# Two transformer blocks on one core: squares summed as tiles become final, the context normed beside an FFN, and a block's start woven tile by tile

## The chip, the core and the metric

The kernel runs on one core of a Trainium2 chip. The metric is the device time of one execution in microseconds (us); a few runs are made and the median is given. Beside the runs stands one profiled execution, from which every row below is read. Engines are written as the profile writes them: PE is TensorE's matmul, PEld its weight load, DVE VectorE, ACT ScalarE, POOL GpSimd, SP SyncE (which issues most transfers). PEclk is TensorE's granted clock as a share of full speed.

## What is computed

One sequence x of 512 tokens and 1024 channels passes through two blocks, all in float32. The first block has four layers, each a mixer and a gated FFN, each behind a root-mean-square norm over the channels:

```
def rmsnorm(x, g):
    return x * rsqrt(mean(x * x, axis=-1) + 1e-6) * g

for i in range(4):          # mixers: hyena, window attention, pooling, hyena
    x = x + mixer_i(rmsnorm(x, norm_mix[i]))
    x = x + (silu(h @ w_gate) * (h @ w_up)) @ w_down      # h = rmsnorm(x, norm_ffn[i])
```

The hyena mixer has a projection, a short convolution, and two long convolutions that are done by Fourier transforms, with the filters' spectra made by a small network. The second block works on x and on a context of 256 further tokens:

```
h  = rms(x,   norm_attn) * (1 + mod_x[1]) + mod_x[0]     # mod_x, mod_c: from c and c_ctx
hc = rms(ctx, norm_attn) * (1 + mod_c[1]) + mod_c[0]
qkv, z, beta, decay, cq, ckv, k_rope, gates = split(h @ w_in)     # the same of hc
o_gdn = gated delta rule, 8 heads, both directions, chunks of 64 tokens
o_mla = softmax attention, 8 heads, keys and values from a low-rank ckv, queries from cq
x = x + mod_x[2] * ((sigmoid(g1) * (o_gdn' @ w_a) + sigmoid(g2) * (o_mla @ w_b)) @ w_out)
x = x + mod_x[5] * (relu(h2 @ w_mlp_in) ** 2 @ w_mlp_out)         # h2: normed and modulated x
```

## The kernel before

Everything is held with channels on the 128 partitions: x is eight tiles `self.x[k]` of [128 channels, 512 tokens] that stay in the on-chip memory. To keep float32 accuracy each operand of a product is split in a high and a low part, and each 128 x 128 block of weights meets a tile of activations in three matmuls (`mm`, lines 383 to 385: high x high, high x low, low x high). A product of one *part*, 128 output channels from eight tiles, is thus 24 matmuls.

Weights come through a plan. Each stage's `plan_...` method lists its requests in the order of their use (`want`, `want_cols`); `part()` takes the next and lets `ahead()` (lines 350 to 375) load the following ones on SyncE's queue and split them: the high part is a cast on ScalarE (L371), the low part a difference on VectorE (L372). There are two buffers for split parts (`look` is 1), so while one is used the next is made. `mark()` ends the stretch of the plan that is loaded ahead before the buffers change size.

The program is written by generators that yield estimates of the TensorE time that they have emitted. `weave` runs several of them side by side, each at an even share of its total, and a scheduler then orders the instructions of each engine by that order and by what is ready.

The stages follow each other: hyena 0, FFN 0 (with the modulation vectors beside it), attention, FFN 1, pooling, FFN 2 (with the second hyena's filters beside it), hyena 3, FFN 3, and `second`, which holds the whole second block: context and x normed, the gate scalars, eight heads of the delta rule (`gdn`), latent attention (`mla`), `merge` and `mlp`.

What the change touches, with the lines of the profile:

- *Norms.* `rstd_g` (L408 to 429) squares eight tiles on ScalarE (L415, L418), adds them on VectorE into `acc` (L419), sums over the channels by a matmul with ones (L422), and takes the root on ScalarE (L425) and the reciprocal on VectorE (L428). The pools of some stages give the sums other names (`raw`, `tmp`, `u`). In the first block `normed` multiplies by the gain at once, and the row factor is wanted only after the first products; in the second block `modulated` (L1151 to 1168) needs the row factor first, then makes each tile by two VectorE instructions and one on ScalarE (L1161, L1165, L1166).
- *Products into x.* `add_to_x` (L501) adds a finished product to x; the FFN's last stretch is eight such products from `hs`, at most eight tiles. L496 is the FFN's gating on GpSimd.
- *Start of the second block.* `second` norms the context first, then x, then runs `both` (a product of a part for x and the context) for a part of 96 columns, turns the result (L1247), computes `gate_scalars` (L1302 to 1349) and only then enters `gdn`. There `front(h)` is a head's projections with short convolution (`gdn_proj`; head 0's keys, values, queries in this order; L1425 turns keys) and `gdn_prep`; `inverse` makes the triangular inverses and `gdn_scan` the recurrence:

```
run(front(0))
weave((self.inverse(tl, own(0, 2), st[0], c), INV + LAG), (front(1), FRONT))
```

- *Last MLP.* `mlp` norms x by `modulated`, then runs 32 parts, of which the squared ReLU goes to the second product.
- *Latent attention.* `keys(hp, out)` makes keys and values of two heads: a product, a norm with a table load on ScalarE (L449), the scaling of each key tile on VectorE (L1767, and the rope part on GpSimd L1768), and the turning of scaled tiles by TensorE (L1776). It is woven with the logits and the values of the heads before (L1837, L1862, L1866).
- *First hyena.* `hyena` opens a pool for the projections and, inside it, the pool of the convolution; L815 loads the spectra `kd` of the filters, L771 stores projections to `vd`, and `kd<-K` is the store of the spectra.

## Time and profile before

| | before |
|---|---|
| median of 3 runs | 4254.73 us (4250.41 to 4256.73) |
| span of the profiled execution | 4239.0 us, 48425 instructions |
| mean granted TensorE clock | 0.962 |
| busy: PE, PEld | 94%, 76% of the span |
| busy: DVE, ACT, POOL | 59%, 37%, 21% |
| DMA | 421.82 MB, mean 100 GB/s |

The span runs from the first to the last instruction of the profiled execution; of that execution only the span is known, and the three runs were made without a profile. A start time in a row is counted from the span's start. Weight loads overlap matmuls, so PE and PEld are not added. In a timeline a bracket behind an instruction gives the idle time of its engine before it and what ended that time.

### The profile page before, as it was taken

The numbers are of one execution on the slowest core, as the hardware profiler recorded it, in microseconds if no ns is written. First come the engines' busy times: TensorE is split into PE (matmuls) and PEld (weight loads), VectorE is DVE, ScalarE is ACT, GpSimd is POOL, SyncE is SP. The second block draws the span as 40 slices with busy tenths as digits, with TensorE's granted clock in tenths as the row PEclk, the third lists the DMA queues.
The fourth block names the chain that finished last, engine by engine and source line by source line (L and its number), as shares of the span: only waits on it lengthen the run. The fifth ranks groups of instructions, "written<-read, shape, count | busy, mean of one in ns | idle before, by whom it ended". The sixth has DMA issues, their size and how long they took to land. (4 is left out here: it accounts for less than half of the span.)

```text
span 4239.0 us, 48425 instructions
## 1 busy us (share of the span) xinstructions
PE 3972.3 (94%) x18340; PEld 3208.1 (76%) x18340; DVE 2511.9 (59%) x4171; ACT 1561.0 (37%) x2858; POOL 896.4 (21%) x977
## 2 busy tenths in 40 slices
PE   7988999989999989998998999689999989998999
PEld 5777788766788777877877888578888876676887
DVE  6766887468544465655666444567777665644333
ACT  4321322257422352323222222454444456643222
POOL 2544101111011102322332111023333321101111
PEclk9999999999999999999999999889999999999999
DMA  4542355230332223334431323222122111242222
GB/s 153 171 172 105 110 189 179 90 102 21 97 97 92 86 87 120 118 116 154 147 122 63 99 90 97 81 63 58 50 65 61 55 45 44 90 134 80 95 94 90
DMA packets 370770, 421.82 MB, mean 100 GB/s; under 512 B 20614, under 2 KB 337046, under 8 KB 365674
## 3 DMA queue, kind: packets, MB, share of 16 engines
q1 hardware_dynamic: 361514, 377.46, 28.1%
q0 software_dynamic: 8736, 40.93, 2.5%
q8 instruction: 144, 2.36, 0.2%
q14 instruction: 88, 0.72, 0.1%
q10 hardware_dynamic: 288, 0.34, 0.0%
HBM read 372.27 MB, written 44.32 MB: 98 GB/s over the span
## 5 line engine op out<-in xcount | busy, mean ns | idle before, releaser
L371 ACT CAST whi<-wraw 128x1024 fp32r<-128x1024 f32 (+4 forms) x546 | 533.3, 977 | 1428.7 <-PE ps L384 1270.3
L383 PE MATMUL ps<-xh,whi 128*128 128x512 f32 x1904 | 787.6, 414 | 15.4 <-ACT whi L371 15.4
L372 DVE TENSOR_TENSOR wlo<-wraw,whi 128x1024 fp32r<-128x1024 f32 (+4 forms) x546 | 676.4, 1239 | 185.0 <-ACT whi L371 165.9
L385 PE MATMUL ps<-xh,wlo 128*128 128x512 f32 x1904 | 760.3, 399 | 1.2 <-DVE wlo L372 1.1
L384 PE MATMUL ps<-xl,whi 128*128 128x512 f32 x1904 | 757.4, 398 | 0.0
L383 PEld LDWEIGHTS ps<-xh,whi 128*128 128x128 f32 x1904 | 361.4, 190 | 101.5 <-ACT whi L371 16.1
L385 PEld LDWEIGHTS ps<-xh,wlo 128*128 128x128 f32 x1904 | 360.2, 189 | 92.2 <-DVE wlo L372 3.7
L384 PEld LDWEIGHTS ps<-xl,whi 128*128 128x128 f32 x1904 | 361.2, 190 | 87.9 <-issue 4.9
L496 POOL TENSOR_TENSOR u<-u,a 128x512 f32<-128x512 f32 x88 | 152.5, 1735 | 1219.2 <-ACT whi L371 737.3
L383 PE MATMUL ps<-hh,whi 128*128 128x512 f32 x960 | 384.5, 400 | 3.0 <-ACT hh L311 3.0
L384 PE MATMUL ps<-hl,whi 128*128 128x512 f32 x960 | 381.0, 397 | 1.0 <-DVE hl L312 1.0
L385 PE MATMUL ps<-hh,wlo 128*128 128x512 f32 x960 | 380.7, 397 | 1.1 <-DVE wlo L372 1.1
L383 PE MATMUL ps<-act,whi 128*128 128x512 f32 (+1 forms) x688 | 291.0, 423 | 9.9 <-ACT act L1165 9.9
L384 PE MATMUL ps<-act,whi 128*128 128x512 f32 (+1 forms) x688 | 284.7, 414 | 1.1 <-DVE act L1166 0.9
L385 PE MATMUL ps<-act,wlo 128*128 128x512 f32 (+1 forms) x688 | 282.4, 411 | 0.0
L501 DVE TENSOR_TENSOR x<-x,ps 128x512 f32<-128x512 f32 x128 | 88.1, 688 | 218.0 <-PE ps L385 217.5
L383 PEld LDWEIGHTS ps<-hh,whi 128*128 128x128 f32 x960 | 180.9, 188 | 47.3 <-ACT hh L311 4.7
L384 PEld LDWEIGHTS ps<-hl,whi 128*128 128x128 f32 x960 | 181.0, 189 | 45.6 <-DVE hl L312 2.4
L385 PEld LDWEIGHTS ps<-hh,wlo 128*128 128x128 f32 x960 | 180.9, 188 | 45.1 <-DVE wlo L372 1.9
L383 PEld LDWEIGHTS ps<-act,whi 128*128 128x128 f32 (+1 forms) x688 | 134.6, 196 | 39.6 <-ACT act L1165 13.3
L574 PE MATMUL ps<-pg,fwd 128*128 128x256 f32 x512 | 133.4, 409 | 30.1 <-DVE pg L564 30.1
L385 PEld LDWEIGHTS ps<-act,wlo 128*128 128x128 f32 (+1 forms) x688 | 134.6, 196 | 30.3 <-issue 0.2
(538 smaller groups left out, 7103.9 us busy)
## 6 DMA issues: line engine op xcount, KB each, us to landing
wraw<-ff_w_gate SPq DMA_DIRECT2D x44, 1024.0 KB
wraw<-ff_w_up SPq DMA_DIRECT2D x44, 1024.0 KB
wraw<-ff_w_down SPq DMA_DIRECT2D x32, 1024.0 KB
wraw<-w_in SPq DMA_DIRECT2D x53, 512.0 KB
wraw<-hy_w_in SPq DMA_DIRECT2D x24, 1024.0 KB
w<-w_mod SPq DMA_DIRECT2D x24, 1024.0 KB
kd<-K POOLq DMA_DIRECT2D x16, 1152.0 KB, 4.8
K<-kd SPq DMA_DIRECT2D x16, 1152.0 KB
```

Of the source, the lines that this page charges most:

```text
L371: nc.scalar.copy(out=hi, in_=src)
L372: nc.vector.tensor_tensor(out=lo, in0=src, in1=hi.bitcast(F32), op=SUB)
L383: nc.tensor.matmul(out[:m, :cols], lhsT=whi[:, k, :m], rhs=xhi[:, :cols], start=(first and k == 0), stop=False)
L384: nc.tensor.matmul(out[:m, :cols], lhsT=whi[:, k, :m], rhs=xlo[:, :cols], start=False, stop=False)
L385: nc.tensor.matmul(out[:m, :cols], lhsT=wlo[:, k, :m], rhs=xhi[:, :cols], start=False, stop=(last and k == nk - 1))
L496: nc.gpsimd.tensor_tensor(out=u, in0=u, in1=a, op=MUL)
L501: self.nc.vector.tensor_tensor(out=self.x[j], in0=self.x[j], in1=ps, op=ADD)
L574: nc.tensor.matmul(ps[:, c, :], lhsT=self.fwd[:, t, s, c, :], rhs=st[t][s], start=(s == 0), stop=(s == 1))
```

## The change

- Each tile of x is squared when it becomes final (`final(j)`): ScalarE squares it, GpSimd adds it to `xsum`, and VectorE adds the last of eight. It is called from the last products of each FFN, the second half of the hyena's and of attention's output, the pooling mixer and the merge. `rstd_g` takes this sum where there is one. The two new tiles take the place of one pair of `h` buffers in FFN 2 (10 instead of 11).
- The context is loaded, normed and modulated by `context`, which runs beside FFN 3; a stage `open_second` before it opens the pools.
- `modulated` becomes a generator, and `modulated_first` takes the first two parts of the plan: it runs the context's products of both, then makes x's tiles one by one and puts the six matmuls of each (two parts, three each) behind it (`mm_k`). In the second block the two parts are the gate scalars' and head 0's keys', which the plan requests early; in the last MLP they are the first two of 32.
- The gate scalars are a generator that is woven with head 0's projections; several small transposes share one copy; the constants are loaded later. `gdn_prep` and `inverse` of head 0 are woven with the whole of head 1's `front`.
- `keys` of latent attention yields 5.0 between the scaling and the turning; the totals of two weaves are 25 and 13 instead of 20 and 10.
- In the first hyena the convolution's pool is opened after the projections' pool is closed.
- Docstrings and comments go; they are left out of the diff below.

```diff
+    def mm_k(self, out, wpart, k, x, last):
+        nc = self.nc
+        (whi, wlo, m), (xhi, xlo) = wpart, x
+        nc.tensor.matmul(out[:m, :], lhsT=whi[:, k, :m], rhs=xhi, start=(k == 0), stop=False)
+        nc.tensor.matmul(out[:m, :], lhsT=whi[:, k, :m], rhs=xlo, start=False, stop=False)
+        nc.tensor.matmul(out[:m, :], lhsT=wlo[:, k, :m], rhs=xhi, start=False, stop=last)
+
+    def final(self, j):
+        nc = self.nc
+        if self.xsums == 0:
+            self.xsum = self.xp.tile([P, T], F32, tag="xsum", name=self.nm("xsum"))
+            nc.scalar.activation(out=self.xsum, in_=self.x[j], func=AF.Square)
+        else:
+            sq = self.xp.tile([P, T], F32, tag="xsq", name=self.nm("xsq"))
+            nc.scalar.activation(out=sq, in_=self.x[j], func=AF.Square)
+            e = nc.vector if self.xsums == KD - 1 else nc.gpsimd
+            e.tensor_tensor(out=self.xsum, in0=self.xsum, in1=sq, op=ADD)
+        self.xsums += 1
+
+    def last_to_x(self, j, ps):
+        self.add_to_x(j, ps)
+        self.final(j)
+
     def rstd_g(self, xs, n, cols=T, tl=None):
...
-        acc = tl("acc", 1)
-        for k, x in enumerate(xs):
+        if xs is self.x and self.xsums == KD:
+            acc, self.xsums = self.xsum, 0
+        else:
+            acc = tl("acc", 1)
+            for k, x in enumerate(xs):
...
-                    hs.append(self.split(pool, u, "h", 11))
-            yield from self.proj(8, hs, self.add_to_x)
+                    hs.append(self.split(pool, u, "h", 10 if li == 2 else 11))
+            yield from self.proj(8, hs, self.last_to_x if g0 + gn == DFF // P else self.add_to_x)
...
+                if first is None:
+                    with self.pool("hy") as pool:
+                        self.hyena_conv(pool, s, first, inputs)
+            if first is not None:
                 with self.pool("hy") as pool:
                     self.hyena_conv(pool, s, first, inputs)
...
-            yield from self.proj(8, zs[k:k + 4], self.add_to_x if k else res)
+            yield from self.proj(8, zs[k:k + 4], self.last_to_x if k else res)
...
-            run(self.proj(8, list(zip(oh_, ol_))[4:], self.add_to_x))
+            run(self.proj(8, list(zip(oh_, ol_))[4:], self.last_to_x))
...
                 nc.vector.tensor_tensor(out=self.x[k], in0=self.x[k], in1=d, op=ADD)
+                self.final(k)
...
-        rstd = self.rstd(x, D, cols=cols)
-        xs = []
+        rstd = yield from self.rstd_g(x, D, cols)
+        xs = [] if xs is None else xs
...
             xs.append((hi, lo))
+            yield 1.0
         return xs
+
+    def modulated_first(self, x, mod, j0, gname, before=()):
+        parts, xs, before = [self.part() for _ in range(2)], [], list(before)
+        ps = [self.psum() for _ in parts]
+        n = 0
+        for _ in self.modulated(self.sx, x, mod, j0, gname, "act", xs=xs):
+            if before:
+                run(before.pop(0)(parts))
+            for k in range(n, len(xs)):
+                for p, part in zip(ps, parts):
+                    self.mm_k(p, part, k, xs[k], k == KD - 1)
+            n = len(xs)
+        return xs, ps
...
         self.want([(w[:, 4768:4832], 0), (w[:, 4096:4128], 64)], KD, 96, [[(0, 96)]])
+        self.want_cols(w, 0, KD, D, P, P)
...
-                if (h < 8) if c < 3 else (h > 0):
+                if (h < 8 and (h or c != 1)) if c < 3 else (h > 0):
...
+    def context(self, pool):
+        cx = []
+        for k in range(KD):
+            t = pool.tile([P, CX], F32, name=self.nm("cx"), tag=f"cx{k}")
+            self.nc.sync.dma_start(out=t, in_=self.i["ctxT"][k * P:(k + 1) * P, :])
+            cx.append(t)
+        yield 1.0
+        self.nt = pool
+        self.cs = yield from self.modulated(self.ctx2, cx, self.modc, 0, "norm_attn_2", "ctx", cols=CX)
+        self.nt = None
...
-            xs = self.modulated(self.sx, self.x, self.modx, 0, "norm_attn_2", "act")
+        with self.norm_pool():
+            pc = [self.psum() for _ in range(2)]
+            xs, px = self.modulated_first(self.x, self.modx, 0, "norm_attn_2",
+                                          [lambda parts, e=e: self.mm(pc[e], parts[e], cs, CX) for e in range(2)])
...
-        run(front(0))
-        weave((self.inverse(tl, own(0, 2), st[0], c), INV + LAG), (front(1), FRONT))
+        weave((self.gate_scalars(b2, lambda: tl([P, 6, P], "w", 7).rearrange("p c d -> p (c d)"), given[0], sc), 30),
+              (self.gdn_proj(tl, own, 0, xs, cs, got, zs, given[1]), 24.0))
...
+        def begin():
+            yield from self.gdn_prep(tl, own, 0, got, st, sc, c)
+            yield from self.inverse(tl, own(0, 2), st[0], c)
+        weave((begin(), 51.0), (front(1), FRONT))
...
         if h < 8:
-            yield from self.both(xs, cs, conv, 0, 2)
+            if given:
+                conv(0, *given)
+            yield from self.both(xs, cs, conv, 1 if given else 0, 1 if given else 2)
             yield from keys()
...
                         g.tensor_scalar(out=kq[:, c, e, :], in0=kr[:, c, :], scalar1=rk[:, c, e:e + 1], scalar2=None, op0=MUL)
+                yield 5.0
                 kT = [tl([P, TT], "kT", 4) for e in range(2)]
...
-            weave((scan, 16.0), (first(), 20.0))
+            weave((scan, 16.0), (first(), 25.0))
...
-                          (values(s - 1, m[(s - 1) // 2], got) if s else None, 8.0), (side, 10.0))
+                          (values(s - 1, m[(s - 1) // 2], got) if s else None, 8.0), (side, 13.0))
...
                                        op0=MUL, op1=ADD)
+                self.final(j)
             run(self.proj(8, zs, res))
...
-            xs = self.modulated(self.sx, self.x, self.modx, 24, "norm_mlp_2", "act")
+            xs, begun = self.modulated_first(self.x, self.modx, 24, "norm_mlp_2")
...
-                run(self.proj(8, xs, relu2))
+                for j, ps in enumerate(begun):
+                    relu2(j, ps)
+                run(self.proj(8 - len(begun), xs, relu2))
+                begun = []
...
-          ("ffn", 2, ("filters", (1,), 140.0)), ("hyena", 3, 1), ("ffn", 3), ("second",))
+          ("ffn", 2, ("filters", (1,), 140.0)), ("hyena", 3, 1), ("open_second",),
+          ("ffn", 3, ("context", (), 20.0)), ("second",))
```

## Rows read from the trace of the kernel before

**Rows 1.** The page: busy time of each engine, and one costly group.

```profile
PE 3972.3 (94%) x18340; PEld 3208.1 (76%) x18340; DVE 2511.9 (59%) x4171; ACT 1561.0 (37%) x2858; POOL 896.4 (21%) x977
...
L501 DVE TENSOR_TENSOR x<-x,ps 128x512 f32<-128x512 f32 x128 | 88.1, 688 | 218.0 <-PE ps L385 217.5
```

**Rows 2.** Waits of TensorE: us in total, times, longest us.

```profile
PE ps L422 <- DVE acc L419: 32.3, 4, 16.9
...
PE ps L1776 <- DVE kk L1767: 12.8, 4, 4.4
```

**Rows 3.** Windows: us; busy PE, PEld, DVE, ACT, POOL; PEclk, DMA, GB/s.

```profile
837.00:868.00 31.00, 31.00 (x134) 24.96 (x133) 17.53 (x23) 12.57 (x16) 0.00 (x0) 1.00 0.35 108
2698.00:2752.00 54.00, 18.09 (x75) 11.28 (x74) 38.61 (x80) 30.49 (x51) 0.87 (x7) 0.71 0.19 50
2776.00:2793.00 17.00, 10.51 (x44) 9.14 (x43) 11.88 (x20) 12.83 (x27) 7.85 (x10) 0.58 0.16 41
2740.00:2793.00 53.00, 37.76 (x181) 32.32 (x181) 32.97 (x78) 35.88 (x72) 8.30 (x18) 0.74 0.33 90
```

**Rows 4.** Timeline from the last FFN to head 0: start, us, instruction.

```profile
2697.94 0.39 PE L385 MATMUL ps<-hh,wlo 128*128 128x512 f32 x1
...
2720.29 2.08 PE L422 MATMUL ps<-acc,ones 128*128 128x512 f32 x2 [16.89 <-DVE acc L419]
...
2723.12 3.35 DVE L428 RECIPROCAL rstd<-sq 128x512 f32<-128x512 f32 x1 [2.89 <-ACT sq L425]
...
2726.51 1.42 DVE L1161 SCALAR_TENSOR_TENSOR t<-x,A,rstd 128x512 f32<-128x512 f32 x2
...
2728.07 0.47 PE L383 MATMUL ps<-act,whi 128*96 128x512 f32 x1 [2.12 <-ACT act L1165]
...
2729.39 1.41 DVE L1161 SCALAR_TENSOR_TENSOR t<-x,A,rstd 128x512 f32<-128x512 f32 x2
...
2751.41 0.56 PE L383 MATMUL ps<-ctx,whi 128*128 128x256 f32 x1
```

**Rows 5.** Single lines: duration in ns (min/median/max), first and last start.

```profile
L418 ACT ACTIVATE sq<-x x28: 612/629/634, 868.5 to 3864.8; 128x512 f32<-128x512 f32 x28
...
L496 POOL TENSOR_TENSOR u<-u,a x88: 1252/1474/2365, 508.0 to 2664.9; 128x512 f32<-128x512 f32 x88
```

**Rows 6.** Timeline: the ones-matmul in attention, pooling and the second hyena.

```profile
880.71 2.08 PE L422 MATMUL ps<-raw,ones 128*128 128x512 f32 x2 [7.38 <-DVE raw L419]
...
1487.14 1.12 PE L422 MATMUL ps<-acc,ones 128*128 128x512 f32 x2 [3.53 <-DVE acc L419]
...
2000.10 2.05 PE L422 MATMUL ps<-tmp,ones 128*128 128x512 f32 x2 [7.19 <-DVE tmp L419]
```

**Rows 7.** The page: weight cast and difference, and the issue of a store.

```profile
L371 ACT CAST whi<-wraw 128x1024 fp32r<-128x1024 f32 (+4 forms) x546 | 533.3, 977 | 1428.7 <-PE ps L384 1270.3
...
L372 DVE TENSOR_TENSOR wlo<-wraw,whi 128x1024 fp32r<-128x1024 f32 (+4 forms) x546 | 676.4, 1239 | 185.0 <-ACT whi L371 165.9
...
kd<-K POOLq DMA_DIRECT2D x16, 1152.0 KB, 4.8
```

**Rows 8.** Timeline: the transposes of head 0's keys.

```profile
2769.91 0.87 PE L1425 MATMUL ps<-ident,c 128*128 128x128 f32 x6
```

**Rows 9.** Timeline: the start of the last MLP on TensorE.

```profile
3866.39 2.08 PE L422 MATMUL ps<-acc,ones 128*128 128x512 f32 x2 [7.55 <-DVE acc L419]
...
3874.17 0.79 PE L383 MATMUL ps<-act,whi 128*128 128x512 f32 x1 [5.71 <-ACT act L1165]
```

**Rows 10.** Timeline: latent attention, the keys of one head pair.

```profile
3551.14 1.28 ACT L449 ACT_TABLE_LOAD   x1
...
3554.11 2.17 PE L1776 MATMUL ps<-ident,kk 128*128 128x128 f32 x6 [4.11 <-DVE kk L1767]
```

**Rows 11.** Timeline: the first hyena, load of the spectra and last store.

```profile
254.76 0.45 SPq L815 DMA_DIRECT2D K<-kd  x1
...
281.19 0.53 POOL L771 DMA_DIRECT2D vd<-st  x1 [3.18 <-DVE st L759]
```

More of the change, by code (lines that the diff above doesn't have):

```diff
@@ L1257, in second @@
         with self.pool("gdn2") as early:
-            low, scan = self.gdn(keep, early, sc, xs, cs, ctx)
+            low, scan = self.gdn(keep, early, tl, xs, cs, ctx, list(zip(px, pc)))
         self.open_psum(2)
@@ L1356, in gdn @@
         c = {}
[L1357 to L1362 removed]
+        got, st, zs, low, sc = {}, {}, {}, [], {}
         def own(h, n):
```

104 lines of the change are left out of this document (48 added, 56 removed).

## Prediction

> **What bounds the kernel now.** I read the page first, then the waits of TensorE, then windows and the timeline at each stage boundary. TensorE is busy for 94% of the span [rows 1]. So the sum is made of the places where it stands still, and of the stretches behind them in which it runs at the lower of its two clocks (1.2 instead of 2.4 GHz), which the windows show. The list of its waits [rows 2] names them: the ones-matmul of a norm waits for the last addition of the squares (32.3 us in four places, one of 16.9), the turned keys of latent attention wait for their scaling (12.8 us in four). Elsewhere TensorE is fed: in the last group of an FFN (the first line of [rows 3]) it is busy for all 31 us, and VectorE and ScalarE have 13 and 18 us to spare. That line also gives the spacing of a full matmul, 31.00 us / 134 = 0.23 us, so the 24 matmuls of one part take 5.6 us and those of half the width, for the context, 2.8 us.
>
> The largest hole lies between the last FFN and head 0 of the delta rule. From 2698 to 2752 us TensorE works 18.1 of 54 us, at a mean clock of 0.71 [rows 3]. The timeline [rows 4] shows one chain: the FFN's last matmul ends at 2698.33 (2697.94 + 0.39); the context's norm and its eight tiles run on VectorE and ScalarE; then come x's squares, whose ones-matmul waits 16.89 us, the reciprocal, x's eight tiles, two in each 2.88 us, with one product of 96 columns behind them, and the gate scalars, some 12 us. Head 0's first product starts at 2751.41, 53 us after the FFN.
>
> **The change part by part.**
>
> *Second block.* The context's norm now runs beside the FFN. It fills no more than the 15 us between 2698.3 and the first square of x, on engines that have a third or more of the FFN's time free: nothing. x's squares are summed as each tile becomes final. Behind the last product there remain: the addition to x 0.69 [rows 1], one square 0.63 [rows 5], one addition of the same shape as the first 0.69, the ones-matmul 1.12 as in the pooling stage [rows 6] (2.08 here, at the low clock), the root with its handovers 0.75 (from 2720.29 + 2.08 to 2723.12), the reciprocal 3.35, and 1.6 us from its end to the first x product [rows 4]. That is 8.8 us, with a few handovers 9.1. In this time TensorE has the context's products of two parts, 5.6 us. Then x's tiles come at 1.44 us each, and the two parts take 6 x 0.23 = 1.4 us of each: 11.5 us. Both are through 21 us after 2698.3. Next comes head 0's value product, whose weights may have to wait until both parts give their buffers free: a cast and a difference, 1.0 and 1.2 us as in rows 7, 2.3 together. With 2.8 + 5.6 us of product and 1 us of small matmuls it ends 21 + 2.3 + 8.4 + 1 = 32.7 us after the FFN. Before, the transposes right behind that product stand at 2769.91 [rows 8], at 71.6 us. So 38.9 us are won here. The gate scalars' 12 us are hidden by the value and query products, 14 us; without that cover they would cost up to 12.
>
> Behind this point, from 2776 to 2793 us, TensorE works 10.5 of 17 us at clock 0.58, some 6 us of work at full clock [rows 3]. This now stands beside head 1's products: up to 11 us more. Against it, ScalarE has 35.9 us of work from 2740 to 2793 [rows 3] and can begin it only at 2719.4; head 0's preparation then ends no earlier than 2755, 38 us before its old place, while TensorE goes on with head 1. I take 42 us for the whole block; bounds 25 (ScalarE in the way) and 48.
>
> *Squares summed early, other norms.* The seven additions behind the last product become one. Attention: TensorE waits 7.38 us at the ones-matmul, which then takes 2.08 us, so the clock had fallen; I take 8 (5.5 to 9.5). Second hyena: 7.19 us and the same slow matmul, 8.5 (5 to 10). Pooling: 3.53 us, 4 (2 to 5.5) [rows 6]. The FFNs use their sums three products late and show no such wait: nothing.
>
> *Last MLP.* TensorE waits 7.55 us for the squares and 5.71 us for the first tile, with a slow ones-matmul of 2.1 us between [rows 9]: 15.3 us. The short chain is 9.1 us, some 9.7 with a weight difference in VectorE's queue, so 5.6 us less, and a microsecond of low clock. Both parts now end together, and the third part's weights (2.3 us as above) can come only then. I take 4.5 (2 to 7).
>
> *Keys turned later.* In three head pairs the scale needs a table load (1.28 us) and small operations, and TensorE waits 4.11 us and the like for the first scaled tile [rows 10]. The added 5.0 puts the transposes behind the logits and values of about a third of a step. What is late next are the keys' copies, which the next step's first logits read; values and queries can lie between. I take 6 us (0 to 14).
>
> *First hyena.* Its convolution pool is opened after the projections' pool is closed, so its tiles may lie where the projections' tiles were. The load of the spectra went out at 254.76; the last store of the projections goes out only at 281.19 [rows 11]. If the load has to wait for that store, it comes 4.8 us after it, as long as a store of the same 1152 KB takes [rows 7], or twice that beside others: up to 9 us late for the first products; if not, it costs nothing, or 2 us are won. I take a loss of 3.
>
> *Squares in the queues.* Nine norms put eight squares on ScalarE and six additions on GpSimd (1.47 us median [rows 5]) into the time of the last products. A product of an FFN's last group lasts 18 x 0.23 = 4.2 us; of that VectorE is busy 2.4 and ScalarE 1.7 us [rows 3], so 0.63 us on ScalarE and 1.47 us on GpSimd fit: nothing. Without that slack a product would be late by the addition and the square, 0.69 + 0.63 = 1.3 us.
>
> Sum: 42 + 8 + 8.5 + 4 + 4.5 + 6 - 3 = 70 us. The profiled execution has a span of 4239.0 us; the median of the three runs, 4254.7, lies 15.7 us above it, which I take as the same afterwards. Predicted: 4254.7 - 70 = 4185 us.
>
> **The rivals.**
>
> *ScalarE becomes the bound of head 0.* The gate scalars need three kinds of function and head 0's convolutions another, and each change loads a table, 1.28 us [rows 10]. Woven, they may need eight loads more, 10 us, and the products no longer cover the chain; 5 us of stalls more behind it. For it: ScalarE's 35.9 us. Against: head 1's products can run meanwhile. 55 us won: 4200. ScalarE: Activation LUTs of the Trainium skill (section "Table sets: the hidden batching unit") warns of just this, calls should be batched by table set; the trace has the loads, but none in two woven streams.
>
> *The keys' wait only moves.* The next heads' logits wait for the late copies as long as the transposes did. 6 us of the sum go, and with them 5 of the block's, if the woven head 1 is short of other work as well: 59 us won, 4196. For it: the transposes lie at the end of their step already. Against: values and queries can go in front.
>
> *Part of it does nothing.* Where the order of the instructions is already mixed, a different order in the program need not change it: matmuls of two parts may alternate already. Then only the context's norm, x's squares and the gates pay, with head 0 alone: 50 us, 4205. Against: nothing of x's norm was early at 2698 us.
>
> *VectorE held by GpSimd.* If VectorE has to stand still while GpSimd adds, it loses 9 x 6 x 1.47 = 79 us, and if TensorE waits for all of it the time is 4254.7 - 70 + 79 = 4264. It decides if VectorE has under 1.5 us of slack for each product; it has 1.8 [rows 3]. SBUF — State Buffer of the Trainium skill (section "Who interferes with whom") says that a VectorE instruction with two inputs in SBUF and a GpSimd one that reads SBUF exclude each other for a whole instruction, which speaks against moving these additions; no row here shows such a pair.
>
> *Slower.* The squares wait in ScalarE's queue for the addition to x, in front of the next weight cast. If each of 72 products (or pooling windows) is late by 1.3 us, 95 us are lost and 70 won: 4280. It decides from 70 / 72 = 0.97 us each. For it: each square does stand in that queue. Against: the slack above.
>
> **How the numbers follow.** The likeliest case 0.6; ScalarE 0.14; keys 0.1; part of it 0.07; VectorE 0.03; slower 0.04; no difference beyond 0.2% (8.5 us, about what a measurement can tell) 0.02. The likeliest one's bounds sum to 30 and 96 us, 4159 to 4224; the terms will not all fall on one side, and with the cases near 4200 the range is 4160 to 4212. Faster 0.91, same 0.02, slower 0.07 (VectorE's case counts as slower).
>
> **What would show it.** In the changed profile the second block's first x product begins some 9 us after the FFN's last matmul; the waits of the ones-matmuls in attention, pooling and the second hyena are under 1.5 us; the MLP's hole is near 10 us; the keys' waits in latent attention are halved; the transposes of head 0's keys stand some 33 us behind the FFN. It would be wrong if the gate scalars show as a wait of 10 us, if the first hyena has a new wait for the spectra, or if the products of an FFN's last group take more than 4.2 us.

## The result and the profile after

The changed kernel takes 4196.63 us (median of four runs, 4191.96 to 4200.14), the kernel before 4252.57 in the same comparison (4249.04 to 4256.73): a ratio of 0.9871, with a 95% interval of 0.9857 to 0.9885, or 49 to 61 us less. 4185 was forecast; the time lies in the range of 4160 to 4212, and of the 70 us that were summed 56 came. The 56 are on the high side: in the four later comparisons the kernel before has medians from 4244.7 to 4247.6, and the changed kernel, taken again, stands 49.6 us below the one beside it.

The two profiled executions differ by less, 4239.0 and 4195.6 us of span, 43.4 us. Every run on record takes 1.7 to 1.9 us more than its span, so the profiled execution of before was one of about 4240.8 us (an estimate), low among its runs, which go from 4233.27 to 4259.17 us in all comparisons. So the terms below are read from the traces, by the start of one and the same instruction in both:

| first or last instruction of its kind | before | after | gained so far |
|---|---|---|---|
| first hyena, first output product | 379.5 | 380.9 | -1.4 |
| first FFN, first product into x | 577.3 | 583.4 | -6.1 |
| attention, first norm of keys | 890.5 | 887.3 | 3.2 |
| pooling, first transpose | 1493.3 | 1486.4 | 6.9 |
| filters beside FFN 2, last product | 1934.1 | 1925.5 | 8.6 |
| second hyena, last inverse transform | 2294.3 | 2277.1 | 17.2 |
| last FFN, last product with x | 2663.1 | 2646.6 | 16.5 |
| second block, first product of x | 2728.1 | 2691.4 | 36.6 |
| head 0, transposes of keys | 2769.9 | 2721.0 | 48.9 |
| head 0, first scan (L1601, now L1671) | 2815.6 | 2786.2 | 29.4 |
| head 7, last matmul with the selector | 3392.6 | 3359.9 | 32.7 |
| merge, first product | 3769.1 | 3731.0 | 38.1 |
| last MLP, last product with x | 4189.3 | 4146.5 | 42.8 |

Two things stand out. The norms give about what was forecast (attention 9.3, pooling 3.7, or 5.4 with what follows, second hyena 8.6, MLP 4.7), and so does latent attention (5.4). The second block wins 32.4 us up to the transposes of head 0's keys and gives 19.5 of them back before head 0's first scan; 16.2 are left at head 7. And 4.7 us are lost where the first FFN starts, which the sum did not have.

The page of the changed kernel (busy time, and the addition of a product to x), which answers to [rows 1]:

```profile
PE 3970.3 (95%) x18340; PEld 3207.3 (76%) x18340; DVE 2502.2 (60%) x4113; ACT 1564.7 (37%) x2859; POOL 979.7 (23%) x1031
...
L532 DVE TENSOR_TENSOR x<-x,ps 128x512 f32<-128x512 f32 x128 | 87.7, 685 | 198.2 <-PE ps L386 197.8
```

The list of TensorE's waits, which answers to [rows 2] (us in total, times, longest us):

```profile
PE ps L1660 <- DVE w L1623: 13.8, 7, 6.6
...
PE ps L1643 <- issue: 6.7, 1, 6.7
PE ps L1493 <- ACT c L1485: 6.6, 1, 6.6
...
PE ps L1847 <- POOL kk L1838: 4.6, 12, 0.5
...
PE ps L453 <- DVE xsum L429: 2.8, 1, 2.8
```

The ones-matmul (now L453) waits once, 2.8 us, where it waited 32.3 us in four places and over 7 us in two more; the turned keys (L1847) wait no longer for VectorE's scaling, which cost 12.8. Three waits of 6.6 to 6.7 us stand in the list that were not there: head 0's next transposes for ScalarE's SiLU (L1493), the first step of the triangular inverse (L1643), and the selector matmul behind the substitution (L1660).

Windows of the changed kernel (us; busy PE, PEld, DVE, ACT, POOL; PEclk, DMA, GB/s): the last group of an FFN, the start of attention, 54 us from the end of the last FFN, and the three new waits:

```profile
837.00:868.00 31.00, 30.78 (x131) 24.29 (x130) 19.12 (x21) 13.95 (x20) 8.42 (x6) 1.00 0.30 92
868.00:885.00 17.00, 17.00 (x70) 12.43 (x69) 11.49 (x11) 7.55 (x9) 3.98 (x5) 1.00 0.50 156
2682.00:2736.00 54.00, 39.28 (x193) 31.78 (x192) 34.60 (x58) 32.90 (x59) 3.40 (x11) 0.87 0.26 72
2728.00:2735.00 7.00, 0.36 (x3) 0.29 (x3) 1.69 (x3) 6.80 (x14) 0.09 (x1) 0.80 0.01 3
2758.00:2765.00 7.00, 0.28 (x2) 0.19 (x2) 3.18 (x4) 0.00 (x0) 3.79 (x3) 0.85 0.04 13
2776.00:2782.00 6.00, 0.00 (x0) 0.00 (x0) 5.79 (x6) 4.65 (x10) 5.36 (x7) 0.83 0.39 105
```

With squares and five of GpSimd's additions in this window of an FFN's last group TensorE stays full (first line, 30.78 of 31 us; VectorE 19.12 where it had 17.53), and attention starts without a hole (second). Behind the last FFN it works 39.3 of 54 us at clock 0.87, where it worked 18.1 at 0.71 [rows 3]. The last three lines are the give-back: TensorE idle, and in each another engine at work, ScalarE for 6.80 of 7 us, then GpSimd (3.79) and VectorE (3.18) one behind the other, then VectorE for 5.79 of 6.

The same stretch in the timeline of the changed kernel, TensorE and the store of the decays on SyncE (start, us, instruction, idle time before it), which answers to [rows 4, 8]; each line is from a window of its own:

```profile
2681.43 0.40 PE L386 MATMUL ps<-hh,wlo 128*128 128x512 f32 x1
...
2684.60 1.12 PE L453 MATMUL ps<-xsum,ones 128*128 128x512 f32 x2
...
2691.43 0.74 PE L394 MATMUL ps<-act,whi 128*96 128x512 f32 x1 [2.87 <-ACT act L1201]
...
2720.98 0.82 PE L1493 MATMUL ps<-ident,c 128*128 128x128 f32 x6
...
2734.71 1.54 PE L1493 MATMUL ps<-ident,c 128*128 128x128 f32 x6 [6.64 <-ACT c L1485]
...
2738.97 0.34 SPq L1410 DMA_DIRECT2D gd<-w  x1
...
2764.84 1.62 PE L1643 MATMUL ps<-Ne,blk 128*128 128x384 f32 x2 [6.72 <-issue]
...
2782.32 1.02 PE L1660 MATMUL ps<-sel,w 128*128 128x8 f32 x4 [6.64 <-DVE w L1623]
```

The FFN ends at 2681.83. The first product of x begins 9.6 us behind it (29.7 before), head 0's keys are turned 39.2 us behind it (71.6 before), the first selector matmul stands at 100.5 us (114.8). The decays, which the triangular matrix of head 0 needs, are stored at 57.1 us. Before the change they were stored at 2753.12, 54.8 us behind the FFN: hidden now, but no earlier.

The give-back has two parts, which the first matmul of the triangular inverse (`ps<-Ne,blk`) divides. Before the change the store of the decays, this matmul and the first selector matmul stood here:

```profile
2753.12 0.34 SPq L1348 DMA_DIRECT2D gd<-gT  x1
...
2800.99 0.81 PE L1573 MATMUL ps<-Ne,blk 128*128 128x384 f32 x2
...
2813.08 1.14 PE L1590 MATMUL ps<-sel,w 128*128 128x8 f32 x9 [1.45 <-issue]
```

Behind the FFN the two matmuls stood at 102.7 and 114.8 us, now at 83.0 and 100.5. From the keys' transposes to the inverse the changed kernel needs 43.9 us instead of 31.1 (12.8 lost), from the inverse to the selector 17.5 instead of 12.1 (5.4 lost), and 1.4 more go up to the scan.

The last MLP, which answers to [rows 9]:

```profile
3823.49 1.17 PE L453 MATMUL ps<-xsum,ones 128*128 128x512 f32 x2 [2.76 <-DVE xsum L429]
...
3830.37 0.79 PE L394 MATMUL ps<-act,whi 128*128 128x512 f32 x1 [5.71 <-ACT act L1201]
```

2.76 + 1.17 + 5.71 = 9.6 us of hole, as the prediction had it (some 9.7).

### The profile page after: what moved, and what is told of

Its sections match the earlier page's. It is cut to its first block, busy times and chain, and to the rows that moved or that the text cites. A ratio compares the mean times of both kernels' runs of the same rounds, so it can differ in the third digit from the quotient of the medians.

```text
span 4195.6 us, 48459 instructions
## 1 busy us (share of the span) xinstructions
PE 3970.3 (95%) x18340; PEld 3207.3 (76%) x18340; DVE 2502.2 (60%) x4113; ACT 1564.7 (37%) x2859; POOL 979.7 (23%) x1031
## 3 DMA queue, kind: packets, MB, share of 16 engines
q1 hardware_dynamic: 361514, 377.46, 28.4%
## 5 line engine op out<-in xcount | busy, mean ns | idle before, releaser
L373 DVE TENSOR_TENSOR wlo<-wraw,whi 128x1024 fp32r<-128x1024 f32 (+4 forms) x546 | 673.2, 1233 | 194.0 <-ACT whi L372 174.4
L384 PE MATMUL ps<-act,whi 128*128 128x512 f32 x656 | 278.4, 424 | 0.2 <-ACT whi L372 0.2
L386 PE MATMUL ps<-act,wlo 128*128 128x512 f32 x656 | 272.3, 415 | 0.5 <-DVE wlo L373 0.5
L385 PE MATMUL ps<-act,whi 128*128 128x512 f32 x656 | 272.5, 415 | 0.0
L532 DVE TENSOR_TENSOR x<-x,ps 128x512 f32<-128x512 f32 x128 | 87.7, 685 | 198.2 <-PE ps L386 197.8
L386 PEld LDWEIGHTS ps<-act,wlo 128*128 128x128 f32 x656 | 129.6, 197 | 29.9 <-DVE wlo L373 1.0
L385 PEld LDWEIGHTS ps<-act,whi 128*128 128x128 f32 x656 | 129.6, 198 | 25.1 <-issue 0.5
```

What stands on the lines that cost most here:

```text
L373: nc.vector.tensor_tensor(out=lo, in0=src, in1=hi.bitcast(F32), op=SUB)
L384: nc.tensor.matmul(out[:m, :cols], lhsT=whi[:, k, :m], rhs=xhi[:, :cols], start=(first and k == 0), stop=False)
L385: nc.tensor.matmul(out[:m, :cols], lhsT=whi[:, k, :m], rhs=xlo[:, :cols], start=False, stop=False)
L386: nc.tensor.matmul(out[:m, :cols], lhsT=wlo[:, k, :m], rhs=xhi[:, :cols], start=False, stop=(last and k == nk - 1))
L532: self.nc.vector.tensor_tensor(out=self.x[j], in0=self.x[j], in1=ps, op=ADD)
```

## Experiments

Three places are compared in every run, always against the first profile of the kernel before: what is won or lost at the first FFN's start (first row to second of the table above), from the last FFN to head 0's first scan, and from head 7 to the merge. Medians are of four to six runs (the second profile of before is one run); single runs of the changed kernel go from 4184 to 4201, so a few us in the total tell little and the places decide.

| kernel | median us | first FFN's start | to first scan | latent attention |
|---|---|---|---|---|
| changed | 4196.6 | -4.7 | 12.9 | 5.4 |
| changed, again | 4198.0 | -4.3 | 12.8 | 7.6 |
| gates_ahead | 4192.4 | -4.8 | 16.9 | 5.0 |
| front2_early | 4207.4 | -4.7 | 10.3 | 5.3 |
| squares_late | 4223.7 | 0.0 | 7.4 | 5.6 |
| squares_vector | 4193.4 | -1.5 | 12.0 | 7.2 |
| keys_back | 4195.5 | -4.7 | 12.9 | 0.0 |
| gates_fewer_tables | 4190.2 | -4.7 | 13.4 | 6.8 |
| prep0_vector | 4196.6 | -4.7 | 17.2 | 6.1 |
| decays_first | 4195.9 | -4.7 | 12.9 | 7.0 |
| combined | 4190.3 | 0.0 | 12.4 | 7.7 |
| ahead_vector | 4184.0 | 0.0 | 16.5 | 5.1 |
| before, again | 4243.3 | 0.4 | -1.4 | -0.1 |

**before_again: how far two profiles of one kernel differ.** No edit.

> The kernel before, unchanged, for a second profile. Its profiled execution had a span of 4239.0 us, while its timed runs had a median of 4252.6. Theory: that execution was a short one; a second profile has a span of 4245 to 4256, and the 6 to 17 us more lie in stretches that can be named. Rival: the span is 4239 again, and 13 us lie outside of it.

The span was 4241.5 us and the one run 4243.26; the runs of before beside it went from 4233.27 to 4253.26. Neither theory is borne out: two profiles lie at 4239 to 4242, the runs around 4246, and only 1.7 to 1.9 us lie outside a span. What does differ is where the time goes. The second profile runs up to 4.6 us ahead of the first, falls back by 6 us between the last FFN and head 7, and ends 2.5 us behind. So two profiles of one kernel differ by some 6 us over the heads, and by 1.4 us at most in the three places of the table. Heads of the delta rule show one reason. Windows of one head each of the changed kernel, and below them of keys_back, with the same instructions:

```profile
3057.40:3144.10 86.70, 82.44 (x486) 72.26 (x485) 59.48 (x139) 40.01 (x95) 28.43 (x34) 0.90 0.19 56
...
3226.10:3308.00 81.90, 77.10 (x485) 67.77 (x485) 59.59 (x139) 39.90 (x96) 29.36 (x31) 0.96 0.20 59
```

```profile
3054.40:3135.00 80.60, 75.85 (x485) 66.65 (x485) 60.13 (x139) 39.66 (x96) 30.17 (x34) 0.98 0.20 60
```

VectorE's and ScalarE's work is the same within about 1%; the granted clock is 0.90, 0.96 and 0.98, TensorE's busy time is 82.4, 77.1 and 75.9 us, and the head takes 86.7, 81.9 and 80.6 us. In all ten such windows of the two kernels the length falls as the granted clock rises. So a head's length goes with the share of time at TensorE's lower level, which one kernel does not repeat from run to run; which of the two sets the other, these windows do not show.

**squares_late: what the early squares are worth.**

```
     def final(self, j):
+        return
```

> No square is taken early; each norm of x squares and adds its eight tiles when it is reached, all else as in the changed kernel. By the offsets of the two traces the early squares won 9.3 us before attention, 4.3 before pooling and 8.6 in the second hyena, lost 4.7 at the start of the first FFN, and save about 6 us of VectorE's additions in front of each of the second block's two norms: 4197 + 9.3 + 4.3 + 8.6 - 4.7 + 12 = 4227, range 4215 to 4235. Rival (the additions on GpSimd and the squares in ScalarE's queue cost as much as they save elsewhere): 4192 to 4205.

4223.7 us, 27.1 above the changed kernel; the rival falls. The first FFN's loss is gone (0.0), and the gains before attention, pooling and the second hyena are gone too: by the last FFN the kernel stands 0.6 us behind the first profile of before, where the changed one stood 16.5 ahead. In the MLP the wait for the squares is back, and the tile-by-tile start without early squares loses 0.9 us there instead of winning 4.7: it wins nothing by itself. Whether the squares would win all of the 4.7 without it, no run shows. Its ones-matmul there in the timeline, as in [rows 9]:

```profile
3848.88 2.08 PE L454 MATMUL ps<-acc,ones 128*128 128x512 f32 x2 [7.54 <-DVE acc L451]
```

**squares_vector: why the first FFN starts late.**

```
-            e = nc.vector if self.xsums == KD - 1 else nc.gpsimd
+            e = nc.vector
```

> All additions of the early squares run on VectorE, none on GpSimd; all else as in the changed kernel. At the start of the first FFN the changed kernel lost 4.7 us against the kernel before, and VectorE's two-input instructions that met one of the six GpSimd additions took about 1.0 us longer (one of 0.48 us took 1.51, a pair of 0.87 took 1.92). Theory (VectorE stands still while GpSimd adds): doing the additions itself costs VectorE some 0.6 us each instead of 1.0, so the loss there falls to 2 to 3.5 us and the whole time is within 3 us of the changed kernel's 4196.6. Rival (GpSimd's additions cost VectorE nothing, the loss has another cause): VectorE gets 3.6 us more to do where it has least to spare, and the loss there grows to 7 to 9 us.

The loss fell from 4.7 to 1.5 us, a little under the 2 to 3.5 expected and far from the rival's 7 to 9; the median is 3.2 us lower, where 3 at most were expected. The timeline of the changed kernel shows what the additions did (POOL L429 is the addition, DVE L1174 the modulation's product, with both inputs in the on-chip memory; DVE L532 adds a product from the matmul's output to x):

```profile
470.39 1.48 POOL L429 TENSOR_TENSOR xsum<-xsum,xsq 128x512 f32<-128x512 f32 x1 [1.95 <-ACT xsq L427]
470.63 1.51 DVE L1174 SCALAR_TENSOR_TENSOR acc<-w,silu_c,acc 128x256 f32<-128x256 f32 x1
...
472.73 0.68 DVE L532 TENSOR_TENSOR x<-x,ps 128x512 f32<-128x512 f32 x1
...
473.93 1.92 DVE L1174 SCALAR_TENSOR_TENSOR acc<-w,silu_c,acc 128x256 f32<-128x256 f32 x2
474.21 1.35 POOL L429 TENSOR_TENSOR xsum<-xsum,xsq 128x512 f32<-128x512 f32 x1 [2.35 <-ACT xsq L427]
```

and the timeline of squares_vector at the same place:

```profile
470.41 0.48 DVE L1174 SCALAR_TENSOR_TENSOR acc<-w,silu_c,acc 128x256 f32<-128x256 f32 x1
470.81 0.68 DVE L429 TENSOR_TENSOR xsum<-xsum,xsq 128x512 f32<-128x512 f32 x1
```

One instruction of 0.48 us takes 1.51 while GpSimd adds, and ends 0.3 us behind GpSimd's; each later pair, triple or four of them beside an addition is longer by about the same 1.0 us (L471, 0.75 us otherwise, by 0.6 and 1.0). Done by VectorE, the addition costs 0.68. It hurts here since the modulation runs beside this stretch: of the 31 us from the hyena's output to the first FFN VectorE was busy 28.38 before the change and had 2.6 to spare, not the 13 of an FFN's last group [rows 3]. Windows of before and, below, of the changed kernel (35.6 us for the same work):

```profile
455.00:486.00 31.00, 30.75 (x120) 23.96 (x120) 28.38 (x51) 16.32 (x25) 1.42 (x2) 0.90 0.34 105
```

```profile
456.40:492.00 35.60, 32.23 (x121) 23.42 (x120) 32.86 (x49) 18.72 (x29) 9.78 (x8) 0.92 0.37 119
```

This is what SBUF — State Buffer of the Trainium skill (section "Who interferes with whom") says of a VectorE instruction with two inputs in SBUF beside a reading GpSimd; the trace agrees, 1.51 against 0.48 us, and L532, with one input from the matmul's output, keeps 0.67 to 0.69 us in the nine places of the trace where GpSimd works beside it. The hold is there in an FFN's last group too: L471 takes 1.28 us beside an addition where it took 0.75, and the slack takes it up.

**keys_back: the later turning of the keys.**

```
-                yield 5.0
                 kT = [tl([P, TT], "kT", 4) for e in range(2)]
...
-            weave((scan, 16.0), (first(), 25.0))
+            weave((scan, 16.0), (first(), 20.0))
...
-                          (values(s - 1, m[(s - 1) // 2], got) if s else None, 8.0), (side, 13.0))
+                          (values(s - 1, m[(s - 1) // 2], got) if s else None, 8.0), (side, 10.0))
```

> The yield in front of the turned keys of latent attention is taken out and the two totals are 20 and 10 again; all else as in the changed kernel. The offsets of the two traces grew by 5.4 us between head 7 of the delta rule and the merge. Theory (the later turning won these): 4 to 7 us slower, 4201 to 4204, and the wait of the turned keys for the scaled tile is back, 12 to 14 us in four places. Rival (the wait had only moved, and the 5.4 us come from the woven totals or from elsewhere): within 2 us of the changed kernel.

The waits are back, in keys_back as in [rows 2]:

```profile
PE ps L1846 <- DVE kk L1837: 12.8, 4, 4.4
```

and the stretch from head 7 to the merge wins 0.0 us, against 5.0 to 7.7 in every other run with the later turning. The median, 4195.5, does not show it: in this profile the heads before ran at a higher clock (19.6 us won at head 7 instead of 16.2). By the place the theory holds, by the total nothing could be said.

**gates_ahead: the gate scalars' place in the weave.**

```
-        weave((self.gate_scalars(b2, lambda: tl([P, 6, P], "w", 7).rearrange("p c d -> p (c d)"), given[0], sc), 30),
+        weave((self.gate_scalars(b2, lambda: tl([P, 6, P], "w", 7).rearrange("p c d -> p (c d)"), given[0], sc), 120),
```

> The gate scalars' share in the weave with head 0's projections is 120 instead of 30, so that they are written ahead of the value and query products. In the changed kernel the store of the cumulated decays went out at 2738.97 us, 57.1 us behind the FFN's last matmul, against 54.8 us before the change (2753.12 against 2698.33): hidden, but not earlier. Theory 1 (the woven gate scalars hold head 0's preparation back): the store goes out at least 6 us earlier, and the time falls by 3 to 7 us against the changed kernel, to 4190 to 4194. Theory 2 (behind the decays, VectorE and GpSimd and the want of products set the pace of head 0): the store is earlier too, but the first matmul with the selector still stands within 2 us of 100.5 us behind the FFN, and the time stays at 4195 to 4199. Rival (TensorE now waits for the gate scalars' own matmuls): 2 to 5 us slower.

The decays are stored at 43.7 us behind the FFN instead of 57.1 (its FFN ends at 2679.89); its timeline on SyncE:

```profile
2723.59 0.34 SPq L1410 DMA_DIRECT2D gd<-w  x1
```

and on TensorE:

```profile
2763.55 0.81 PE L1643 MATMUL ps<-Ne,blk 128*128 128x384 f32 x2
...
2774.41 1.50 PE L1660 MATMUL ps<-sel,w 128*128 128x8 f32 x12 [0.62 <-DVE w L1623]
```

The selector matmul comes at 94.5 us, 6.0 earlier, and the first scan has won 16.9 instead of 12.9 us. The forecast of theory 1 came, but not by its mechanism: with the decays 13.4 us earlier the inverse begins at 83.7 us, not before the 83.0 of the changed kernel (its operand is ready 1.9 us earlier, at 81.0, and then other products are still in front of it on TensorE). All that is won lies behind it, where the selector follows after 10.9 instead of 17.5 us. What VectorE did in between, in the changed kernel (L1483 is the convolution and L1588 the decays of head 1, L373 weights, L1623 head 0's own):

```profile
L1483 DVE SCALAR_TENSOR_TENSOR c<-c,vecs,c 128x770 f32<-128x770 f32 x6 | 6.1, 1017 | 0.2 <-ACT c L1481 0.2
L1588 DVE SCALAR_TENSOR_TENSOR D<-D,gc,neg 128x128 f32<-128x128 f32 x8 | 4.3, 541 | 0.0
L1623 DVE TENSOR_TENSOR w<-t,blk 128x768 f32<-128x768 f32 x1 | 2.6, 2608 | 0.0
L373 DVE TENSOR_TENSOR wlo<-wraw,whi 128x1024 fp32r<-128x1024 f32 x2 | 2.5, 1226 | 0.3 <-ACT whi L372 0.2
```

and in gates_ahead:

```profile
L1483 DVE SCALAR_TENSOR_TENSOR c<-c,vecs,c 128x770 f32<-128x770 f32 x7 | 7.1, 1018 | 0.1
...
L373 DVE TENSOR_TENSOR wlo<-wraw,whi 128x1024 fp32r<-128x1024 f32 x1 | 1.2, 1219 | 0.0
L1623 DVE TENSOR_TENSOR w<-t,blk 128x768 f32<-128x768 f32 x1 | 1.0, 953 | 0.0
```

VectorE is busy nearly all the time in both. Head 1's decays now stand in front of the inverse, one of two differences of weights is gone, and head 0's own last step is no longer stretched. So head 0's substitution waits in VectorE's queue behind head 1's work. That is read from the traces; no run takes head 1's work out.

**gates_fewer_tables: is it ScalarE's tables?** In `gate_scalars` the functions are replaced:

```
-        nc.scalar.activation(out=beta, in_=tok[:, :, 64:80], func=AF.Sigmoid)
+        nc.scalar.activation(out=beta, in_=tok[:, :, 64:80], func=AF.Copy)
...
-        nc.scalar.activation(out=g, in_=u, func=AF.Ln)
+        nc.scalar.activation(out=g, in_=u, func=AF.Copy)
```

> The gate scalars' sigmoid and logarithm are replaced by copies, so their values are others and two to three table loads of 1.28 us fall away on ScalarE; all else as in the changed kernel. Rival of the prediction (ScalarE's table loads set the pace of head 0): the time falls by 3 to 5 us. Theory (the order in which the instructions stand in the queues sets it, the decays come late since their first copy waits behind the convolution on VectorE and their sums behind a product on TensorE): the store of the decays is less than 4 us earlier and the time falls by less than 2 us.

From the FFN's end to the selector the profile holds 10 table loads; the changed kernel has 13 and the kernel before 12. Three loads less (3.8 us) make the store of the decays 1.3 us earlier and the first scan 0.5. The whole fell by 6.5 us, which the place does not explain and the runs' spread does.

**front2_early: more products to cover the chain.**

```
+        f2 = front(2)
-        weave((begin(), 51.0), (front(1), FRONT))
+        weave((begin(), 51.0), (chain(front(1), some(f2, 12.0)), FRONT + 12.0))
```

`some` takes the first 12.0 of a generator; in the weave of head 0's scan `f2` goes on with FRONT - 12.

> While head 0 is prepared and inverted, the first 12 us of head 2's projections are written beside head 1's, and head 2's later share is that much smaller. In the changed kernel TensorE stands still for 6.64, 6.72 and 6.64 us between 2728 and 2783 us. Theory 2 (head 1's products alone don't cover head 0's chain): the last of these gaps, and perhaps the second, are filled, and the time falls by 5 to 12 us, to 4185 to 4192. Theory 1 (the chain starts too late, and what fills it now is missing in the next stretch): the gaps only move behind the first scan; within 3 us of 4197. Rival (more convolutions in VectorE's queue lengthen the substitution): the chain ends 3 us or more later and the time rises by up to 5.

10.8 us slower, more than any theory gave. TensorE's waits in its timeline:

```profile
2728.38 0.90 PE L1503 MATMUL ps<-ident,c 128*128 128x128 f32 x3 [6.63 <-ACT c L1495]
...
2761.52 0.90 PE L1503 MATMUL ps<-ident,c 128*128 128x128 f32 x3 [8.30 <-ACT c L1495]
...
2782.48 0.69 PE L1681 MATMUL ps<-S,w 128*128 128x8 f32 x5 [3.31 <-DVE S L1644]
...
2822.46 0.44 PE L1681 MATMUL ps<-w,w 128*128 128x64 f32 x1 [4.36 <-DVE w L1644]
```

The holes do not close, they move: the inverse begins at 89.9 us behind the FFN instead of 83.0, the first scan has won 10.3 us, head 1's first scan only 0.2 (18.5 in the changed kernel), and by head 7 2.6 of 16.2 us are left. By the program every product brings a convolution for VectorE and ScalarE, so products are no free cover; that this is what costs head 0's scan ten us is argued, not shown.

**prep0_vector: five of GpSimd's instructions out of head 0's preparation.** With gates_ahead; the masked products of `inverse` stay on GpSimd:

```
-        v, a, g = nc.vector, nc.scalar, nc.gpsimd
+        v, a, g = nc.vector, nc.scalar, nc.gpsimd if h else nc.vector
```

> The gate scalars are written ahead as in the run of that name, and head 0's five elementwise products and sums of its preparation run on VectorE instead of GpSimd. With the scalars ahead the decays were stored 13.4 us earlier against the FFN's last matmul, but the first matmul with the selector came only 6.0 us earlier; four VectorE instructions of 0.34 us took 5.34 us while GpSimd worked on the triangular matrix, and the reduction waited for GpSimd. Theory (GpSimd holds VectorE and stands in head 0's chain): the first selector matmul comes 3 to 6 us earlier than with the scalars ahead alone, the time falls by 2 to 5 us to 4187 to 4191. Rival (VectorE has no room, the chain only changes engines): within 1.5 us of 4192.

The selector matmul comes at 94.8 us instead of 94.5, the first scan has won 17.2 us instead of 16.9, and head 1's first scan 19.5 against 22.2, of which the clock may have a part. By the place the rival holds: the preparation changes engines and keeps its length. The median, 4196.6, is 4 us above gates_ahead, where neither theory had it; the runs' spread is of that size.

**decays_first: the order in ScalarE's queue.** With gates_ahead, head 0's exponentials are written ahead of its products of keys:

```
+        def decays(d):
+            col = 8 * d + h
+            Dm, qd = D2[d], own(h, 2)([P, T], "qd", 2)
+            a.activation(out=qd, in_=Dm[:, 2:6, :].rearrange("p c d -> p (c d)"), func=AF.Exp)
...
+            a.activation(out=Dm, in_=Dm, func=AF.Exp)
+            return qd
+        early = [decays(d) for d in range(2)] if h == 0 else None
         KK, QK = tl([P, 6, P], "w", 7), tl([P, 4, P], "QK", 1)
```

> The gate scalars are written ahead as in the run of that name, and head 0's decays and their exponentials are written in front of the products of its keys instead of behind them. With the scalars ahead alone, the decays had arrived at 2729.3 us but the exponential of the second direction ended at 2752.7, behind ScalarE's other work and two changes of its table, and the first selector matmul came 94.4 us behind the FFN's last matmul (100.5 in the changed kernel). Theory 1 (the order of the queues sets head 0's chain): the first selector matmul comes 3 to 7 us earlier than 94.4. Theory 2 (VectorE's and GpSimd's work on the triangular matrix sets it): within 2 us of 94.4. The whole time moves by less than the runs differ among each other, so the place of the selector matmul decides.

The selector matmul came at 100.1 us, and the 4 us of gates_ahead were gone (12.9 again). Both theories miss: the order does matter, but the other way. The copies of the key products then stand behind the exponentials on ScalarE, 5 to 6 us later, but the inverse begins only 0.6 us later (84.3). The loss lies behind it again: 15.8 us to the selector instead of 10.9, with GpSimd busy for 6.2 of them instead of 2.7 and more of head 1's work in VectorE's queue.

**combined, after_again and ahead_vector.** combined is gates_ahead, decays_first, squares_vector, and in the first hyena:

```
-            yield from self.proj(8, zs[k:k + 4], self.last_to_x if k else res)
+            yield from self.proj(8, zs[k:k + 4], self.last_to_x if k and s else self.add_to_x if k else res)
```

> The scalars ahead, head 0's decays first, the squares' additions all on VectorE, and no early squares in the first hyena's last products. Sum of the single runs' places: 4.0 us at head 0 from the scalars ahead, 0 to 5 from the decays, 3.2 at the start of the first FFN from VectorE's additions and about 1.5 more from leaving them out there: 8 to 13 us less than the changed kernel in the same call, 4180 to 4190. Rival (the pieces fill the same idle time): 0 to 5 us less.

> The changed kernel, unchanged, beside the two others for a comparison on one chip, and for a second profile. Expected within 5 us of 4196.6, and its stretch from the last FFN to head 0's first scan the same to 1 us as in the first profile (12.9 us gained against the kernel before), since that stretch was alike in every kernel that shares its code; the time of the heads behind it follows the granted clock, 80.6 us at 0.98 and 86.7 at 0.90.

combined took 4190.3 us beside 4198.0 of the changed kernel: 7.7 us, just under the 8 to 13 expected. The first FFN's loss is gone, head 0 has not gained (12.4). after_again repeated the first scan's place to 0.1 us (12.8), while at head 7 it had won 13.4 us instead of 16.2. ahead_vector is combined without decays_first:

> The combined run without the decays in front: the scalars ahead, the squares' additions on VectorE, no early squares in the first hyena's last products. With the scalars ahead alone head 0's first scan had gained 16.9 us against the kernel before, counted from the last FFN, with the decays first as well 12.9 and 12.4 (the changed kernel: 12.9 and 12.8). If the decays in front undo the gain of the scalars, as these places say, the first scan gains 16 to 18 us here, the first FFN's start loses less than 0.5 us, and the time is 6 to 12 us below the changed kernel's 4197, 4185 to 4191. If the 4.0 us were chance, the first scan gains 12 to 14 us.

Its selector matmul in the timeline, 95.7 us behind its FFN:

```profile
2767.33 1.40 PE L1660 MATMUL ps<-sel,w 128*128 128x8 f32 x12
```

16.5 us at the first scan, 0.0 at the first FFN, 4184.0 us (4178.31 to 4186.55), the fastest kernel here and one us below the expected 4185 to 4191: ratio to before 0.9854 (0.9833 to 0.9875). Against the changed kernel that is 12 to 14 us by the medians, of which 4.7 + 3.6 = 8.3 are shown by places; the rest is not. The 3.6 tell chance from effect: without the decays in front the gain of the scalars is back.

## Why the prediction was right, and where it was not

- *Direction, range and most terms* held. Attention: 8 forecast, 9.3 found. Second hyena 8.5 and 8.6. Pooling 4 and 3.7 (3.3 to 5.8 in the other runs with early squares), or 5.4 with the FFN behind it. MLP 4.5 and 4.7 (2.6 to 4.7), though squares_late shows that the woven start wins nothing by itself. Latent attention 6 and 5.4 (5.0 to 7.7 over the runs), with VectorE's waits gone. That the total lies in the range though the largest term fell short by 26 us is owed to the range, which leaves 27 us on that side for cases that did not come.
- *The sum* was made against a profile 15.7 us below the median of its runs, and that distance was taken as lasting. The profile after lies 1.0 us below its own median. So the places of this pair add up to 43.4 us where 70 were summed; the remaining 12.6 of the 56 measured have no place in these two traces. Some 6 of them are the high median of the kernel before in that comparison (49.6 us the second time).
- *The second block* was the term that was mis-sized: 42 forecast, 16.2 found (13.4 in the second profile, and two profiles of the kernel before differ by 6 us over this stretch), below the bound of 25. Its first half was right: 9.1 us to the first product of x, 9.6 found, the same to 0.1 us in every run with early squares. No run undoes this part; it is read from the timelines. The keys' transposes came 6.5 us later than worked out (39.2 instead of 32.7): both parts were through at 22.6 us instead of 21, the next weights kept TensorE waiting 2.64 + 2.52 us instead of 2.3, behind the convolution in VectorE's queue, and the context's matmuls behind that wait came 0.21 us apart instead of 0.12, at a clock of 0.79.

  The step that failed is the next one: "head 0's preparation then ends no earlier than 2755, 38 us before its old place, while TensorE goes on with head 1", from which "up to 11 us more" were counted. The bound was made from ScalarE's amount of work alone, and head 1 was taken as cover that costs head 0 nothing. The inverse came 19.7 us before its old place, not 38, and instead of up to 11 us won 19.5 were given back. "The gate scalars' 12 us are hidden" is true, though they end no earlier than before (57.1 us behind the FFN instead of 54.8), and they are not what held head 0: 13.4 us earlier, they moved the inverse's operand by 1.9 us and the inverse by nothing. Behind the inverse the loss of 5.4 us goes with head 1's work in VectorE's queue (convolution, decays and weights, 12.9 us of it between inverse and selector, 8.3 in gates_ahead, 5.3 before). Of the 12.8 us in front of it fewer tables won 0.8 us; GpSimd's five instructions moved, another order and the decays earlier won none, and more products lost 6.9. Which link of the preparation would have to be shortened stays open.
- *First FFN.* "Squares in the queues: nothing" was read from an FFN's last group. At the first hyena's end the modulation fills VectorE, and there the same edit cost 4.7 us, 3.2 of them by GpSimd's additions. The rival "VectorE held by GpSimd" had the right mechanism, at 0.6 to 1.0 us for each of six additions in the one place without slack instead of 79 us in nine.
- *First hyena.* A loss of 3 was forecast for its pools. Its condition came true: the first load of the spectra went out at 286.04 us instead of 254.76, behind the last store (282.88). But the wait of the convolution's start is 7.48 us in both traces, and the offset of 1.4 us is within what two profiles of one kernel differ by (3.5 there).
- *Other rivals.* "ScalarE becomes the bound" named 55 us in all, close to the result by chance: its eight more loads were one more, and three less gave 0.5 us at the first scan. The rule of ScalarE: Activation LUTs of the Trainium skill (section "Table sets: the hidden batching unit"), that calls be batched by table set, finds hardly a price at this place, 0.5 us for three loads. "The keys' wait only moves" and "part of it does nothing" fell, the last but for the MLP's start.

## What to carry to other kernels

Work that covers a wait of one engine is work for the others: head 1's products fed TensorE, and its convolution and decays stood in VectorE's queue in front of head 0's substitution. For a moved chain, ask of each engine on it what else stands in its queue, and not only how much work one of them has. And what is made earlier need not be what was waited for: the decays came 13.4 us earlier and the inverse behind them did not. Slack is that of the place: the same six additions cost 4.7 us with their squares at one norm, where VectorE was busy 28.4 of 31 us, and no more than about one us could be told at any other. When runs scatter by ten us, compare the start of one instruction in two traces, stretch by stretch, and leave the total for the sum.

## What the runs showed of the hardware

A VectorE instruction with two inputs in the on-chip memory stood still while GpSimd added two tiles: 1.51 instead of 0.48 us. Each of six additions in a row held one so, for 0.6 to 1.0 us, and none did when VectorE made the additions; nine instructions with one input from the matmul's output kept their 0.67 to 0.69 us beside GpSimd. One head of the delta rule, with the same instructions, took 80.6 us at a granted clock of 0.98 and 86.7 at 0.90, and which head got which clock changed from execution to execution.
